# Stick-breaking attention: the weights' small parts on GpSimd by slices, another order of the k products, and the last two key blocks transposed as one group

## The chip, the core and the metric

The kernel runs on one core of a Trainium2 chip. The metric is the device time of one execution in microseconds. The numbers of the trace are those of one profiled execution, from its first to its last instruction. TensorE is PE in the rows (PEld its weight load), VectorE DVE, ScalarE ACT, GpSimd POOL, SyncE SP.

## What is computed

One layer of a macaron block on x of 1024 rows by 1024 columns, in float32: half a SwiGLU feed-forward, stick-breaking attention, half a SwiGLU feed-forward, each with an RMS norm ahead and added to x. The change lies in the attention, with 16 heads of 64 columns:

```python
qkv = (xn @ w_qkv).reshape(b, s, 3, SB_HEADS, SB_HEAD_DIM)
q = rms_norm(qkv[:, :, 0], q_gain).transpose(0, 2, 1, 3)
k = rms_norm(qkv[:, :, 1], k_gain).transpose(0, 2, 1, 3)
v = qkv[:, :, 2].transpose(0, 2, 1, 3)
...
z = jnp.einsum('bhqd,bhkd->bhqk', q[:, :, lo:hi], k[:, :, :hi]) * scale
log_beta = jax.nn.log_sigmoid(z)
log_1m = jnp.where(mask, jax.nn.log_sigmoid(-z), 0.0)
rev = lax.cumsum(log_1m, axis=3, reverse=True)
...
w = jnp.where(mask, jnp.exp(log_beta + rev_excl), 0.0)
outs.append(jnp.einsum('bhqk,bhkd->bhqd', w, v[:, :, :hi]))
```

## The kernel before

Every product in float32 is made of three matmuls of rounded operands: an operand is split into its large part (a copy by ScalarE into the rounded type) and its small part (the operand minus the large part, by VectorE or GpSimd; `split`, L167 to L169). The rows of x are taken in reverse, so a query sees keys from itself onward.

The attention goes pair of heads by pair of heads, p from 0 to 7, after a start that is counted as pair -1. Of a pair there are four units, a head (`hd`, 0 or 1) and a half of 512 queries (`half`). For each unit the scores and the weights are made (`scores`, L747: score matmuls, two sigmoids by ScalarE, a scan by VectorE, a product by GpSimd in L780), and one unit later the weights are transposed and multiplied with v (`values`, L784). `values` takes the key blocks sb from the last to the first: `turn` transposes up to four 128x128 blocks of weights into one PSUM bank and splits them into `th` and `tl`; `apply` multiplies each of the two with v's block into one bank, `bo`. A unit of the later half has 4 key blocks, one of the earlier half 8. The last key block has one 128x128 block of weights, its matmul is 256 wide all the same, and the second 128 columns of `th` and `tl` are set to zero by GpSimd (L801).

Beside the units of pair p run the steps of pair p + 1: its q, k and v (`qkv`, 24 steps of nine matmuls, half 1 first, then half 0), and the loads and splits of the weights of pair p + 2 (`weights_of`: a step loads two 128-row blocks of 384 columns, ScalarE copies 768 columns, GpSimd subtracts 768 columns in one instruction, L659 through L169). When the fourth block of a half is done, `finish` makes the norms' factors (`rsqrt`, VectorE) and GpSimd scales k: the slots 0 and 1 of `qk` are the two heads' q, the slots 2 and 3 their k. L705 writes the second head's k, scaled, into the slots 4 and 5 (512 columns in one instruction), then L708 writes the first head's k into 3 and into 2 (256 columns each). `prep_q` and `prep_k` transpose the slots (`turned_qk`, L725): the first head's keys come from the slots 2 and 3, the second head's from 4 and 5.

The order comes from a plan written out by hand: a pair has 61 units of planned time in four parts a, b, c and d (`PARTS`), every step has a due time, and the steps are traced in the order of these times. From that order the instruction order of each engine is laid out before the run, where an instruction that is expected to be ready may be placed ahead of an earlier one that is not. It is fixed at run time: each engine works its queue in order. In the plan the steps of `qkv` are spread by `FILLS` over the parts; a unit's `turn` steps start 4.0 after a part's start (`TURN`) and each `apply` is due 2.3 after its `turn` (`APPLY`); the keys of the first head and half 0 are due at a + 7.5, those of the second head at b + 8.0, those of half 1 at c + 17.5 and d + 8.0; the weights' steps are due at a + 6, b + 8, d + 2 and d + 8. In pair 6 the mark at d + 16.5 is the place by which the output projection's loads and splits are ordered; they are on SyncE's queue, ScalarE, VectorE and GpSimd.

Of the kernel before, what the change touches and what calls it, by code (L numbers as in the profile page):

```python
# [9 lines left out]
F32 = mybir.dt.float32  # L10
# [7 lines left out]
P = 128  # L18
# [20 lines left out]
PARTS = {"a": 9.0, "b": 14.0, "c": 21.0, "d": 17.0}  # L39
# [4 lines left out]
FILLS = {"a": 3, "b": 6, "c": 8, "d": 7}  # L44
# [54 lines left out]
def macaron_kernel(ctx, tc, x, g1, w1_in, w1_out, gm, w_qkv, gq, gk, w_o, g2, w2_in, w2_out, out):  # L99
# [535 lines left out]
    with ExitStack() as stack:  # L635
# [9 lines left out]
        def weights_of(p, state):  # L645
# [3 lines left out]
            def step(k):  # L649
# [9 lines left out]
                split(raw.rearrange("p k a c -> p k (a c)"), h_[:, ks], l_[:, ks], pool_e)  # L659
                for i in range(2):  # L660
                    wh[k + i], wl[k + i] = h_[:, k % 4 + i, :], l_[:, k % 4 + i, :]
# [3 lines left out]
        def qkv(p, state):  # L665
# [20 lines left out]
            def finish(half, i, ps, room):  # L686
# [16 lines left out]
                rk = r[:, :, 1:2].unsqueeze(3).to_broadcast([P, 4, 2, DH])  # L703
                kv = qk[:, :, 3:4, :].to_broadcast([P, 4, 2, DH])
                pool_e.tensor_tensor(qk[:, :, 4:6, :], kv, rk, op=ALU.mult)  # L705
                for to in (3, 2):
                    rk = r[:, :, 0:1].to_broadcast([P, 4, DH])
                    pool_e.tensor_tensor(qk[:, :, to, :], qk[:, :, 2, :], rk, op=ALU.mult)  # L708
# [31 lines left out]
        def prep_k(state, hd, half):  # L740

            kh_s, kl_s = state["k", hd, half] = [
                pl[f"st{half}"].tile([P, NHALF], F32R, name=f"k{n}_s{half}") for n in "hl"
            ]
            parts(turned_qk(state["qk", half], 2 + 2 * hd), g_sb[1], kh_s, kl_s)
# [38 lines left out]
        def values(state, p, hd, half):  # L784
# [5 lines left out]
            def turn(sb):  # L790
                w = state["w", hd, half]
                n_tb = min(4, sb - tb0 + 1)
                n = n_tb * P
                tp = bank("bt")
                for i in range(n_tb):
                    c = (sb - tb0 - i) * P
                    pe.transpose(tp[:, i * P : (i + 1) * P], w[tb0 + i][:, c : c + P], ident)
                th, tl = now[sb] = [pl["th"].tile([P, NHALF], F32R, name=n) for n in ("th", "tl")]
                if n_tb == 1:
                    for t in (th, tl):  # L800
                        pool_e.memset(t[:, P : 2 * P].bitcast(F32), 0.0)  # L801
                split(tp[:, :n], th[:, :n], tl[:, :n])

            def apply(sb):
                if hd == 0 and sb == NT - 1:
                    state["o", half] = pl["o"].tile([P, NHALF], F32, name=f"o{half}", bufs=1)
                if sb == NT - 1:
                    now["o"] = bank("bo")
                ot = now["o"]
                n = max(min(4, sb - tb0 + 1), 2) * P  # L810
                vv = state["v"][:, sb, 2 * hd : 2 * hd + 2, :].rearrange("p a b -> p (a b)")
                for i, t in enumerate(now.pop(sb)):
# [211 lines left out]
```

## Time and profile before

| | us |
|---|---|
| median of 3 runs | 2016.31 |
| lowest, highest | 2014.38, 2016.91 |
| the profiled execution | 2019.49 |
| its span, first to last instruction | 2017.7 |
| mean granted TensorE clock in it | 0.988 |

The profiled execution has an own time, 1.8 us more than its span. Sums of rows are set against it. In the span the attention's steps run from about 690 to 1316 us, and the pairs 1 to 5, which have all kinds of steps, repeat every 70 to 71 us. A row of a timeline gives in brackets how long the engine was idle before the instruction, and which instruction released it. The granted clock is 1.00 at 2.4 GHz and 0.50 at 1.2 GHz.

### The profile page before, as it was taken

How to read it: one execution, taken by the hardware profiler on the slowest of the kernel's cores; microseconds unless marked ns; L12 is line 12 of the kernel's file. 1: busy time of each engine (PE TensorE's matmuls, PEld its weight loads, DVE VectorE, ACT ScalarE, POOL GpSimd, SP SyncE). 2: the span in 40 equal slices, each digit the busy share in tenths (PEclk: the TensorE clock that was granted, in tenths of full speed). 3: DMA queues.
4: the chain of work that ended last, by engine and by line, in shares of the span. 5: the costliest groups of instructions: out<-in, count | busy, mean ns of one | idle time of the engine just before them, and what ended most of it. 6: DMA issues, size and time to landing. Idle time of an engine off the chain costs nothing.

```text
span 2017.7 us, 27277 instructions
## 1 busy us (share of the span) xinstructions
PE 1926.7 (95%) x9624; PEld 1649.5 (82%) x9624; DVE 1259.7 (62%) x1815; ACT 987.2 (49%) x1828; POOL 1106.3 (55%) x957
## 2 busy tenths in 40 slices
PE   7899999999999789889988998999999999999999
PEld 6788888887888689888888986779888888888887
DVE  6945645636666847767767777567564564547654
ACT  6443443443334457767776777443434334344332
POOL 2567667656456434654555456312766666655554
PEclk9999999999999999999999999999999999999999
DMA  5123233338996410110011013232233233259974
GB/s 204 65 97 111 104 100 103 111 115 294 332 320 222 126 32 6 43 37 27 22 43 32 6 58 126 65 124 69 96 113 100 100 115 99 94 188 360 317 267 150
DMA packets 163031, 251.85 MB, mean 125 GB/s; under 512 B 10960, under 2 KB 80592, under 8 KB 162896
## 3 DMA queue, kind: packets, MB, share of 16 engines
q1 hardware_dynamic: 162896, 250.13, 36.5%
q8 instruction: 75, 1.23, 0.3%
q14 instruction: 60, 0.49, 0.1%
HBM read 193.99 MB, written 56.10 MB: 124 GB/s over the span
## 4 chain that ended last, share of the span: by engine, by line
PE 79%; DVE 10%; POOL 4%; ACT 4%; issue 2%; DMA 1%; POOLq 0%; DVEq 0%; ACTq 0%
PE ka L255 6%; PE ka L256 6%; PE ka L257 6%; PE kc L255 4%; PE kc L256 4%; PE kc L257 4%; PE bq L257 4%; PE bq L255 4%; PE bq L256 4%; PE ma L255 4%; PE ma L256 4%; PE ma L257 4%; PE kb L256 3%; PE kb L255 3%; PE kb L257 3%; PE bo L813 3%
## 5 line engine op out<-in xcount | busy, mean ns | idle before, releaser
L169 POOL TENSOR_TENSOR u<-sf,u 128x512 fp32r<-128x512 f32 x160 | 226.6, 1417 | 160.9 <-ACT u L168 160.1
L169 POOL TENSOR_TENSOR rp<-raw,rp 128x1024 fp32r<-128x1024 f32 x84 | 213.1, 2542 | 184.5 <-ACT rp L168 166.2
L169 POOL TENSOR_TENSOR u<-raw,u 128x512 fp32r<-128x512 f32 x136 | 201.1, 1483 | 147.3 <-ACT u L168 147.2
L780 POOL TENSOR_TENSOR w<-w,om 128x512 f32<-128x512 f32 (+4 forms) x128 | 138.7, 1086 | 134.0 <-DVE om L773 111.1
L168 ACT ACTIVATE u<-sf 128x512 fp32r<-128x512 f32 x160 | 100.9, 630 | 217.8 <-PE kb L256 89.8
L363 DVE TENSOR_TENSOR h<-h 128x512 f32<-128x512 f32 x110 | 134.7, 1228 | 90.0 <-POOL h L464 89.3
L255 PE MATMUL bq<-wqh,xh 128*128 128x384 f32 x512 | 179.2, 350 | 3.8 <-DVE vst L694 3.8
L256 PE MATMUL bq<-wql,xh 128*128 128x384 f32 x512 | 174.2, 340 | 0.0
L257 PE MATMUL bq<-wqh,xl 128*128 128x384 f32 x512 | 173.8, 339 | 0.0
L168 ACT ACTIVATE rp<-rh 128x1024 fp32r<-128x1024 f32 (+1 forms) x78 | 76.6, 984 | 198.6 <-issue 70.8
L255 PE MATMUL ka<-xh,u 128*128 128x512 f32 (+1 forms) x448 | 163.0, 364 | 9.8 <-ACT s L413 7.6
L256 PE MATMUL ka<-xl,u 128*128 128x512 f32 (+1 forms) x448 | 162.8, 364 | 1.2 <-DVE xl L169 1.2
L257 PE MATMUL ka<-xh,u 128*128 128x512 f32 (+1 forms) x448 | 162.3, 362 | 0.0
L485 DVE TENSOR_TENSOR raw<-raw 128x1024 f32<-128x1024 f32 (+1 forms) x60 | 91.0, 1519 | 111.1 <-DMA raw<-w_out 91.0
L168 ACT ACTIVATE u<-raw 128x512 fp32r<-128x512 f32 x136 | 84.6, 631 | 148.2 <-PE ka L256 101.8
L255 PE MATMUL ma<-rp 128*128 128x512 f32 x352 | 138.0, 392 | 2.0 <-DVE h L417 2.0
L771 ACT ACTIVATE w<-bz,f 128x512 f32<-128x512 f32 (+1 forms) x192 | 113.0, 589 | 52.4 <-PE bz L767 50.4
L256 PE MATMUL ma<-rp 128*128 128x512 f32 x352 | 137.6, 391 | 0.0
L257 PE MATMUL ma<-rp 128*128 128x512 f32 x352 | 137.4, 390 | 0.0
L390 DVE TENSOR_TENSOR sf<-raw 128x512 f32<-128x512 f32 x80 | 79.1, 990 | 89.3 <-POOL u L169 88.1
L464 POOL TENSOR_TENSOR h<-h,g 128x512 f32<-128x512 f32 x80 | 112.1, 1401 | 29.0 <-DVE h L417 29.0
L169 DVE TENSOR_TENSOR tl<-bt,th 128x512 fp32r<-128x512 f32 x192 | 103.3, 548 | 33.6 <-ACT th L168 32.8
(220 smaller groups left out, 5584.4 us busy)
## 6 DMA issues: line engine op xcount, KB each, us to landing
raw<-w_out SPq DMA_DIRECT2D x120, 512.0 KB, 5.5
raw<-w_in SPq DMA_DIRECT2D x88, 512.0 KB, 3.6
k<-h SPq DMA_DIRECT2D x154, 256.0 KB, 2.1
rh<-k SPq DMA_DIRECT2D x64, 512.0 KB, 5.8
raw_qkv<-w_qkv SPq DMA_DIRECT2D x64, 192.0 KB, 2.9
x_keep<-x SPq DMA_DIRECT2D x32, 256.0 KB, 2.5
x<-x_keep SPq DMA_DIRECT2D x32, 256.0 KB, 5.0
raw<-w_out SPq DMA_DIRECT2D x24, 256.0 KB, 4.2
```

The source lines that it names most:

```text
L168: act.activation(hi, raw, AF.Copy)
L169: (engine or dve).tensor_tensor(lo, raw, hi.bitcast(F32), op=ALU.subtract)
L255: pe.matmul(dst, ah, bh, start=start and i == 0, stop=False, skip_group_check=onto)
L256: pe.matmul(dst, ah, bl, start=False, stop=False, skip_group_check=onto)
L257: pe.matmul(dst, al, bh, start=False, stop=stop and i == n - 1, skip_group_check=onto)
L363: dve.tensor_tensor(src, hb[of[0]], hb[of[1]], op=getattr(ALU, of[2]))
L390: dve.tensor_tensor(f[n], x, y, op=op)
L464: pool_e.tensor_tensor(h, h, gs[k], op=ALU.mult)
L485: dve.tensor_tensor(w[0], w[0], w[1], op=getattr(ALU, W_OF[m][2]))
L771: act.activation(to, z, AF.Sigmoid, scale=state["f", half][:, sign, tb % 4, hd : hd + 1])
L780: pool_e.tensor_tensor(wt[:, c1 : c0 + n], wt[:, c1 : c0 + n], om[:, c1 - 1 : c0 + n - 1], op=ALU.mult)
L813: pe.matmul(ot[:, :n], vv, t[:, :n], start=sb == NT - 1 and i == 0, stop=sb == tb0 and i == 1)
```

## The change

The constants of the plan: part a gets 10 units instead of 9 and part d 16 instead of 17; a has 4 steps of `qkv` instead of 3 and d has 6 instead of 7. In `weights_of` ScalarE's copy stays one instruction of 768 columns, and GpSimd's subtraction becomes two of 384 columns, each for its own 128-row block. In `finish` the roles of the slots are exchanged: the first instruction (512 columns) now scales the first head's k into the slots 4 and 5, the two of 256 columns scale the second head's k into 2 and 3; `prep_k` takes the slots accordingly. In `values` the last two key blocks form one group: their transposes (two and one, and one of a block of zeros from the tile `first`) go into one bank, one split makes `th` and `tl` of 512 columns, and the four matmuls follow one another. The memsets are gone. A unit has 3 or 7 groups instead of 4 or 8, and the due times of its groups are spread over that number.

```diff
--- before.py
+++ after.py
@@ -36,12 +36,12 @@
 
 
 
-PARTS = {"a": 9.0, "b": 14.0, "c": 21.0, "d": 17.0}
+PARTS = {"a": 10.0, "b": 14.0, "c": 21.0, "d": 16.0}
 PAIR = sum(PARTS.values())
 UNITS = {"a": (1, 1), "b": (0, 0), "c": (1, 0), "d": (0, 1)}
 BEFORE = {"a": (0, 1), "b": (1, 1), "c": (0, 0), "d": (1, 0)}
 
-FILLS = {"a": 3, "b": 6, "c": 8, "d": 7}
+FILLS = {"a": 4, "b": 6, "c": 8, "d": 6}
 
 LOADS = (("a", 6.0), ("b", 8.0), ("d", 2.0), ("d", 8.0))
 
@@ -656,8 +656,11 @@
                 for i in range(2):
                     sp.dma_start(raw[:, i], src[:, i, :, p * P : (p + 1) * P])
                 ks = slice(k % 4, k % 4 + 2)
-                split(raw.rearrange("p k a c -> p k (a c)"), h_[:, ks], l_[:, ks], pool_e)
+                raw = raw.rearrange("p k a c -> p k (a c)")
+                act.activation(h_[:, ks], raw, AF.Copy)
                 for i in range(2):
+                    k_ = k % 4 + i
+                    pool_e.tensor_tensor(l_[:, k_, :], raw[:, i, :], h_[:, k_, :].bitcast(F32), op=ALU.subtract)
                     wh[k + i], wl[k + i] = h_[:, k % 4 + i, :], l_[:, k % 4 + i, :]
 
             return [partial(step, k) for k in ((4, 6, 0, 2) if p == 0 else (0, 2, 4, 6))]
@@ -700,12 +703,12 @@
                 r = pl["sq"].tile([P, 4, 4], F32, name="r", bufs=1)
                 dve.tensor_scalar(r[:, :, 0:2], y[:, :, 2:4], 1.0, None, op0=ALU.mult)
 
-                rk = r[:, :, 1:2].unsqueeze(3).to_broadcast([P, 4, 2, DH])
-                kv = qk[:, :, 3:4, :].to_broadcast([P, 4, 2, DH])
+                rk = r[:, :, 0:1].unsqueeze(3).to_broadcast([P, 4, 2, DH])
+                kv = qk[:, :, 2:3, :].to_broadcast([P, 4, 2, DH])
                 pool_e.tensor_tensor(qk[:, :, 4:6, :], kv, rk, op=ALU.mult)
-                for to in (3, 2):
-                    rk = r[:, :, 0:1].to_broadcast([P, 4, DH])
-                    pool_e.tensor_tensor(qk[:, :, to, :], qk[:, :, 2, :], rk, op=ALU.mult)
+                for to in (2, 3):
+                    rk = r[:, :, 1:2].to_broadcast([P, 4, DH])
+                    pool_e.tensor_tensor(qk[:, :, to, :], qk[:, :, 3, :], rk, op=ALU.mult)
 
                 f = state["f", half] = pl["sq"].tile([P, 2, 4, 2], F32, name=f"f{half}")
                 for n, c in enumerate((0.125, -0.125)):
@@ -742,7 +745,7 @@
             kh_s, kl_s = state["k", hd, half] = [
                 pl[f"st{half}"].tile([P, NHALF], F32R, name=f"k{n}_s{half}") for n in "hl"
             ]
-            parts(turned_qk(state["qk", half], 2 + 2 * hd), g_sb[1], kh_s, kl_s)
+            parts(turned_qk(state["qk", half], 4 - 2 * hd), g_sb[1], kh_s, kl_s)
 
         def scores(state, hd, half):
 
@@ -787,31 +790,39 @@
             tb0 = half * 4
             now = {}
 
-            def turn(sb):
+            def blocks(sb):
+                return min(4, sb - tb0 + 1)
+
+            def turn(sbs):
                 w = state["w", hd, half]
-                n_tb = min(4, sb - tb0 + 1)
-                n = n_tb * P
                 tp = bank("bt")
-                for i in range(n_tb):
-                    c = (sb - tb0 - i) * P
-                    pe.transpose(tp[:, i * P : (i + 1) * P], w[tb0 + i][:, c : c + P], ident)
-                th, tl = now[sb] = [pl["th"].tile([P, NHALF], F32R, name=n) for n in ("th", "tl")]
-                if n_tb == 1:
-                    for t in (th, tl):
-                        pool_e.memset(t[:, P : 2 * P].bitcast(F32), 0.0)
+                n = 0
+                for sb in sbs:
+                    for i in range(max(blocks(sb), 2)):
+                        c = (sb - tb0 - i) * P
+
+                        src = w[tb0 + i][:, c : c + P] if i < blocks(sb) else first[:, P : 2 * P]
+                        pe.transpose(tp[:, n : n + P], src, ident)
+                        n += P
+                th, tl = now[sbs] = [pl["th"].tile([P, NHALF], F32R, name=n) for n in ("th", "tl")]
                 split(tp[:, :n], th[:, :n], tl[:, :n])
 
-            def apply(sb):
-                if hd == 0 and sb == NT - 1:
+            def apply(sbs):
+                if hd == 0 and sbs[0] == NT - 1:
                     state["o", half] = pl["o"].tile([P, NHALF], F32, name=f"o{half}", bufs=1)
-                if sb == NT - 1:
+                if sbs[0] == NT - 1:
                     now["o"] = bank("bo")
                 ot = now["o"]
-                n = max(min(4, sb - tb0 + 1), 2) * P
-                vv = state["v"][:, sb, 2 * hd : 2 * hd + 2, :].rearrange("p a b -> p (a b)")
-                for i, t in enumerate(now.pop(sb)):
-                    pe.matmul(ot[:, :n], vv, t[:, :n], start=sb == NT - 1 and i == 0, stop=sb == tb0 and i == 1)
-                if sb > tb0:
+                c = 0
+                ts = now.pop(sbs)
+                for sb in sbs:
+                    n = max(blocks(sb), 2) * P
+                    vv = state["v"][:, sb, 2 * hd : 2 * hd + 2, :].rearrange("p a b -> p (a b)")
+                    for i, t in enumerate(ts):
+                        start, stop = sb == NT - 1 and i == 0, sb == tb0 and i == 1
+                        pe.matmul(ot[:, :n], vv, t[:, c : c + n], start=start, stop=stop)
+                    c += n
+                if sbs[-1] > tb0:
                     return
                 o = state["o", half]
                 act.activation(o[own, :], ot[other, :], AF.Copy)
@@ -821,8 +832,8 @@
                 elif hd == 1 and (p, half) != (NP - 2, 1):
                     split_o(state, p, half)
 
-            sbs = range(NT - 1, tb0 - 1, -1)
-            return [(partial(turn, sb), partial(apply, sb)) for sb in sbs]
+            groups = [(sb,) for sb in range(NT - 1, tb0 + 1, -1)] + [(tb0 + 1, tb0)]
+            return [(partial(turn, sbs), partial(apply, sbs)) for sbs in groups]
 
         def split_o(state, p, half):
```

## Rows read from the trace of the kernel before

**Rows 1.** The page, part 1: busy us (share of the span) xinstructions.

```profile
PE 1926.7 (95%) x9624; PEld 1649.5 (82%) x9624; DVE 1259.7 (62%) x1815; ACT 987.2 (49%) x1828; POOL 1106.3 (55%) x957
```

**Rows 2.** Stretches: us, busy us (x) of PE, PEld, DVE, ACT, POOL, PEclk, DMA.

```profile
821.00:892.40 71.40, 64.03 (x384) 58.74 (x384) 51.72 (x104) 50.58 (x114) 39.46 (x62) 1.00 0.11 32
```

**Rows 3.** Waits of PE, 700 to 1316: who, whom, us, times, longest.

```profile
PE bz L725 <- POOL qk L708: 20.9, 8, 3.6
PE bo L813 <- POOL tl L801: 9.7, 6, 1.9
...
PE bo L813 <- DVE tl L169: 2.9, 8, 0.6
```

**Rows 4.** Timeline of PE: start us, us, instruction [idle before, releaser], 881 and 892.

```profile
881.24 0.39 PE L813 MATMUL bo<-tl,vst 128*128 128x256 f32 x1 [1.56 <-POOL tl L801]
...
892.78 0.47 PE L725 MATMUL bz<-ident,qk 128*128 128x128 f32 x1 [3.64 <-POOL qk L708]
```

**Rows 5.** Timeline of POOL, 879 to 893, the same columns.

```profile
879.21 1.80 POOL L169 TENSOR_TENSOR wql<-raw_qkv,wqh 128x768 fp32r<-128x768 f32 x1
...
888.50 1.81 POOL L169 TENSOR_TENSOR wql<-raw_qkv,wqh 128x768 fp32r<-128x768 f32 x1
890.27 1.05 POOL L705 TENSOR_TENSOR qk<-qk,r 128x512 f32<-128x512 f32 x1
891.40 0.62 POOL L708 TENSOR_TENSOR qk<-qk,r 128x256 f32<-128x256 f32 x1
```

**Rows 6.** Timeline of DVE, at 887.

```profile
887.44 0.17 DVE L701 TENSOR_SCALAR r<-bq 128x8 f32<-128x8 f32 x1
```

**Rows 7.** Timeline of PE at the keys of four other pairs.

```profile
750.13 1.12 PE L725 MATMUL bz<-ident,qk 128*128 128x128 f32 x4 [4.04 <-POOL w L778]
...
822.94 0.66 PE L725 MATMUL bz<-ident,qk 128*128 128x128 f32 x4 [3.64 <-POOL qk L708]
...
964.17 0.70 PE L725 MATMUL bz<-ident,qk 128*128 128x128 f32 x3 [3.61 <-POOL qk L708]
...
1174.41 0.65 PE L725 MATMUL bz<-ident,qk 128*128 128x128 f32 x4 [1.45 <-POOL qk L708]
```

**Rows 8.** Stretches after a wait, columns as in rows 2 (PEclk: granted clock).

```profile
749.38:756.20 6.82, 6.07 (x22) 5.90 (x23) 1.30 (x3) 1.45 (x4) 2.23 (x7) 0.50 0.22 60
892.74:896.15 3.41, 3.37 (x14) 3.28 (x15) 1.26 (x3) 1.56 (x4) 1.17 (x4) 0.50 0.16 46
822.90:826.30 3.40, 3.36 (x23) 3.24 (x24) 1.28 (x3) 1.34 (x4) 1.60 (x5) 1.00 0.16 45
1234.08:1240.90 6.82, 5.44 (x19) 4.93 (x20) 4.03 (x7) 4.80 (x8) 6.82 (x7) 0.50 0.88 317
```

**Rows 9.** Groups of DVE by shape, 700 to 1316: xcount, busy us, mean ns, idle.

```profile
L773 DVE TENSOR_TENSOR_SCAN om<-bz,om,first 128x512 f32<-128x512 f32 x64 | 82.1, 1282 | 25.0 <-ACT bz L771 22.9
L169 DVE TENSOR_TENSOR tl<-bt,th 128x512 fp32r<-128x512 f32 x96 | 63.8, 682 | 13.4 <-ACT th L168 13.4
```

**Rows 10.** Transposes of PE: their group by shape, then four in a row (timeline).

```profile
L797 PE MATMUL bt<-ident,w 128*128 128x128 f32 x576 | 98.4, 275 | 1.5 <-POOL w L780 1.2
...
872.11 0.60 PE L797 MATMUL bt<-ident,w 128*128 128x128 f32 x4
```

**Rows 11.** Timeline of POOL, 745 to 749.

```profile
745.99 1.05 POOL L705 TENSOR_TENSOR qk<-qk,r 128x512 f32<-128x512 f32 x1
746.99 1.81 POOL L169 TENSOR_TENSOR wql<-raw_qkv,wqh 128x768 fp32r<-128x768 f32 x1
```

**Rows 12.** Groups of POOL by shape, 700 to 1316, columns as in rows 9.

```profile
L780 POOL TENSOR_TENSOR w<-w 128x383 f32<-128x383 f32 x16 | 16.1, 1008 | 10.8 <-DVE w L773 10.8
```

**Rows 13.** Timeline of PE in the last pair.

```profile
1232.97 0.39 PE L813 MATMUL bo<-th,vst 128*128 128x256 f32 x1 [1.64 <-POOL th L801]
...
1235.46 0.58 PE L813 MATMUL bo<-tl,vst 128*128 128x256 f32 x1 [1.87 <-POOL tl L801]
...
1261.60 0.79 PE L256 MATMUL bq<-pa,xh 128*128 128x512 f32 x1 [2.18 <-POOL w L778]
```

## The prediction

> **What bounds the kernel now.** The page's first part comes first: TensorE is busy 95% of the span, the other engines 49 to 62% [rows 1]. So a change that touches GpSimd alone can only pay where TensorE stands still for it. The diff lies in the attention stage, where the heads' pairs follow each other at a fixed pace; in one pair of 71.4 us TensorE is busy 64.0, VectorE 51.7, ScalarE 50.6 and GpSimd 39.5 [rows 2]. The waits of TensorE in the stage name the causes [rows 3]: 20.9 us in 8 waits for the k products (L708), 9.7 us in 6 waits for the memset of the small half (L801). Waits for VectorE's splits are small, 2.9 us in 8.
>
> The timeline shows both in every steady pair, at the same places. Near the end of a unit the last matmul stands 1.56 us before 881.24, and the next pair's first keys stand 3.64 us before 892.78, so from 889.14 [rows 4]. Behind the first lies GpSimd's order: a weights' subtraction of 1.80 us started at 879.21, and the second memset had to wait for its end at 881.01 [rows 5]. Behind the second lies the same: the factors r were ready at 887.44 + 0.17 = 887.61 [rows 6], but a subtraction of 1.81 us began at 888.50, the second head's product (L705, 1.05 us) at 890.27 only, and the first head's two products of 0.62 us followed it, with a 1-column memset between, to 892.72 [rows 5].
>
> **A check that such waits are TensorE's own time.** The keys' wait ends at 822.94, 892.78, 964.17 and 1174.41 in four of the pairs [rows 4, 7]. From 892.78 to 964.17 is 71.4 us, but the last three pairs took 210.2, that is 4.0 less than 3 x 71.4. In the last of them the keys' wait is 1.45 and not 3.64 (2.2 less), and none of the six memset waits lies there (1.56 less): 3.7 of the 4.0. Time taken off these waits comes out at the end.
>
> **The clock behind the waits.** After the wait at 892.78 the granted clock is 0.50 for 3.4 us (1.2 instead of 2.4 GHz), at 749.38 for 6.8; after the equal wait at 822.94 it stayed at 1.00 [rows 8]. What this costs is the difference of two otherwise equal pairs: 892.78 - 822.94 = 69.84 without it and 71.39 with it, so 1.55 us; the pair from 750.13 to 822.94 took 72.81, so 3.0 us for the longer one. Four steady pairs pay 1.55.
>
> **The change, part by part.** The terms are gains, in us of the profiled execution.
>
> Memsets out, last two key blocks together. 64 memsets go from GpSimd. The wait of 1.56 was for one, in 5 steady pairs: 5 x 1.56 = 7.8. What is late next there is the small half from VectorE. The merged group is of the 512-column form, which 96 groups already take at 0.68 us on VectorE [rows 9], planned the same 2.3 units (2.7 us) ahead of its matmuls; all waits for VectorE's small halves sum to 2.9 [rows 3]. 32 more such groups: 32 x 2.9 / 96 = 1.0 lost. The worst of these waits was 0.6, so the bounds are 0 and 20 lost; I take 1.0, since it is the mean of the same form.
> Each of the 32 units (16 heads, two halves) gets one more transpose, of zeros, on TensorE. Four in a row take 0.60, and one alone 0.275 from start to end [rows 10], so (0.60 - 0.275) / 3 = 0.11 each: 3.5 lost, all of it on the path. The Trainium skill, "TensorE: Matmul & The Clock Gate", Part 4, gives about 275 ns for a 128x128 transpose in a kernel. That agrees with one instruction's length here (0.275), and by it the loss would be 8.8 and the time 5 us more; but starts lie 0.11 apart, so the row decides.
>
> First head's k first. Its keys need L705's place alone (1.05) and no longer 1.05 + 2 x 0.62. At 750.13 L705 had started at 745.99 and ended at 747.04, and a subtraction of 1.81 from 746.99 then held up the other two [rows 11]; TensorE came at 750.13 - 4.04 = 746.09 [rows 7], so 1.0 is left: 3.0 gained. At 1174.41 no subtraction is near, and the wait of 1.45 [rows 7] is that of the two products (1.24) and little else: 1.3 gained. Of 20.9 - 5 x 3.63 - 1.45 = 1.3 in the remaining two waits I take 1.0. The second head's keys come later by two small products, but their step is due about 10 plan units after the first's, so those 1.24 us are covered.
>
> Weights slice by slice. No row has the slice itself; the nearest is the product of 383 columns, 1.01 us [rows 12], so two slices take 2.02 where one instruction took 1.80 to 1.85 [rows 5]: 0.2 us more GpSimd time, 32 times, off the path but for the place below. ScalarE's copy and the DMAs stay as they are. In the five steady pairs the subtraction ahead of L705 decides. If both slices stay ahead, the keys come at 888.50 + 2.02 + 1.05 = 891.57 and TensorE, there at 889.14, waits 2.5. If L705 passes the second slice, 1.5. With no slice ahead, near 0. I take 2.0, the middle of the first two, as the order is fixed ahead by expected times and r came only 0.9 ahead of the subtraction: 5 x (3.63 - 2.0) = 8.2, between 5.7 and 18. Sum of the keys' waits: 3.0 + 1.3 + 1.0 + 8.2 = 13.5.
>
> The clock. A wait of 1.0 is shorter than the 1.56 that did not lower it, so 3.0 comes back at 749.38. Waits of 1.5 to 2.5 lie between that and the 3.6 that lowered it in four of five pairs; I take half of 4 x 1.55: 3.1. Together 6.1, bounds 0 and 9.2.
>
> The last pair's start. Two memset waits, 1.64 and 1.87 [rows 13], and 6.8 us at half clock [rows 8] are worth 3.5 + 3.0 = 6.5. But there the output weights' splits fill the other engines and TensorE soon waits for them again, 2.18 at 1261.60; and with a of 10 and d of 16 the mark at d + 16.5 from which those splits and their DMAs are ordered falls one unit (1.2 us) later. I take half: 3.2, bounds 0 and 6.5.
>
> Shifted plan. a grows by a unit and d shrinks, one filling step moves from d to a, and a unit's groups go from 4 or 8 to 3 or 7. Between the last filling step of d and the keys' step of a, three filling and three score steps remain; one turn less and one apply more weigh each other out. Cost nothing, covered by TensorE's own queue; without that cover a shift of a group is some tenths in a pair.
>
> Sum: 7.8 - 1.0 - 3.5 + 13.5 + 6.1 + 3.2 = 26.1. The profiled execution took 2019.5 (span 2017.7 and 1.8 around it), so 1993.4; it lies 0.16% over the median of 2016.3, so 1990 us.
>
> **The rivals.**
> 1. GpSimd's order does not let the first head's keys out earlier: other work takes the freed place, the steady pairs keep 3.6 and the half clock. Then 8.2 and 3.1 fall away: 26.1 - 11.3 = 14.8, some 2001 us. For it: lower work has slipped ahead of these products in every pair. Against: two products of 0.62 no longer stand before those keys, whatever the order.
> 2. More than forecast: L705 ahead of all slices, no wait and no half clock left, the last pair's whole 6.5: 26.1 + 10 + 3.1 + 3.3 = 42.5, some 1974 us. For it: r is ready at 887.61, ahead of the subtraction. Against: the order is fixed before r is known.
> 3. The time is given back: without its waits a pair would be near 66 us, VectorE 51.7 / 66 = 78% busy [rows 2], and the in-order queues of VectorE and ScalarE set the pace at more places. Price: the 26 less a few, some 2012 us, within 0.2%. Against: the pair up to 1174.41 ran at 67.4 with no new wait.
> 4. Slower. The merged group puts all four last matmuls behind one split, which waits for both blocks. If VectorE has one more 512-column scan ahead of the small half (1.28 us [rows 9]) than TensorE has work to cover, each of the 32 units stands for it: 32 x 1.28 = 41, 2016 - 26 + 41 = 2031 us. It decides from 26 / 32 = 0.8 us a group, over the 0.6 that is the worst wait for a small half so far [rows 3]. For it: VectorE is the second busiest in a pair [rows 2]; against: the 96 groups of that form.
>
> **How the numbers follow.** Chances: forecast 0.48 (its own range 1982 to 2000, by the order of the slices and the clock), rival 1 0.20, rival 2 0.10, rival 3 0.12, rival 4 0.10. The range of 1974 to 2010 takes in the forecast, rivals 1 and 2 and the better part of rival 3. Faster by over 0.2% (which is about what can be told from no change) is under 2012.3: 0.48 + 0.20 + 0.10 + 0.03 = 0.81; within it 0.09; slower 0.10.
>
> **What would show it.** In the trace after, no wait for L801; where the unit's last matmuls stood, at most 0.6 for VectorE. The keys' wait between 1.5 and 2.5 in five pairs, after one or two 384-column subtractions of 1.0, and released by the product of 512 columns. A distance of 66 to 67 us between those waits. Half clock in at most two or three pairs, and none near 750. 608 transposes of blocks instead of 576. The forecast is wrong if the keys' wait stays near 3.6, if waits for the merged small half exceed 0.6, or if the distance of the pairs stays over 69.

## The result and the profile after

The changed kernel takes 2000.2 us (median of 4 runs, 1998.8 to 2000.7) against 2016.6 for the kernel before on the same chip: a ratio of 0.9913, 95% interval 0.9898 to 0.9928. The profiled execution took 2000.7 us with a span of 1998.7, where the one before had 2019.5 and 2017.7: 18.8 us less by execution. Forecast were 1990 us and 26.1 us less. In the changed kernel the product of 512 columns is L708, the two small ones are L711, the keys are turned at L728, memset and product of the weights are L781 and L783, the group is turned at L805 and applied at L823.

The page, part 1 (busy us, share of the span, instructions), answering [rows 1]: 32 matmuls more, 32 instructions fewer on VectorE, ScalarE and GpSimd each.

```profile
PE 1928.4 (96%) x9656; PEld 1651.5 (83%) x9656; DVE 1260.4 (63%) x1783; ACT 988.3 (49%) x1796; POOL 1100.9 (55%) x925
```

The waits of TensorE from 700 to 1316 us, answering [rows 3] (who, for whom, us in total, times, longest):

```profile
PE bz L728 <- POOL qk L708: 12.2, 6, 2.4
PE bq L257 <- POOL w L781: 4.1, 1, 4.1
PE bt L805 <- POOL w L783: 3.6, 9, 1.2
...
PE bo L823 <- DVE tl L169: 1.6, 5, 0.6
PE bo L823 <- ACT th L168: 1.5, 1, 1.5
```

No wait for a memset of the small half is left (9.7 us before), nor the 1.6 for one of the large half. The keys are waited for 12.2 us instead of 20.9 and the 4.0 at 750 us. Waits for VectorE's small halves fell from 2.9 to 1.6. Against that stand waits that are new or have grown: 1.5 for ScalarE's large half, 4.1 in the last pair (0.6 before), 3.6 in nine waits for GpSimd's product of the weights, L783 (1.2 in one before), and three new ones of 0.4 to 0.8. At the keys, timeline of TensorE and then of GpSimd (start, us, instruction, idle before and releaser), answering [rows 4, 5, 7]:

```profile
740.41 0.49 PE L823 MATMUL bo<-th,vst 128*128 128x512 f32 x1 [1.47 <-ACT th L168]
...
879.23 0.66 PE L728 MATMUL bz<-ident,qk 128*128 128x128 f32 x4 [2.30 <-POOL qk L708]
```
```profile
877.17 1.00 POOL L663 TENSOR_TENSOR wql<-raw_qkv,wqh 128x384 fp32r<-128x384 f32 x1
878.12 1.05 POOL L708 TENSOR_TENSOR qk<-qk,r 128x512 f32<-128x512 f32 x1
879.13 1.01 POOL L663 TENSOR_TENSOR wql<-raw_qkv,wqh 128x384 fp32r<-128x384 f32 x1
880.09 1.33 POOL L711 TENSOR_TENSOR qk<-qk,r 128x256 f32<-128x256 f32 x2
```

The product of 512 columns stands between the two slices, and the keys are released by it. The stretches behind these waits, answering [rows 8] (us, busy us of PE, PEld, DVE, ACT, POOL, then the granted clock):

```profile
742.16:745.57 3.41, 3.41 (x16) 3.41 (x15) 3.35 (x7) 3.04 (x8) 3.41 (x7) 0.50 0.39 112
810.43:813.84 3.41, 3.41 (x14) 3.41 (x15) 1.86 (x4) 1.60 (x4) 2.80 (x5) 0.50 0.29 82
878.70:882.10 3.40, 2.87 (x20) 2.87 (x21) 2.39 (x6) 1.73 (x5) 3.32 (x7) 1.00 0.27 79
...
1216.62:1226.86 10.24, 6.78 (x24) 5.49 (x24) 7.71 (x18) 4.14 (x9) 7.88 (x10) 0.50 0.92 329
1240.51:1247.34 6.83, 6.13 (x18) 4.89 (x18) 3.02 (x5) 1.84 (x4) 3.30 (x5) 0.50 0.44 148
```

Behind the shorter waits the clock is still 0.50 (1.2 instead of 2.4 GHz) at 810, 947, 1015 and 1083 us, at 1.00 only at 879; in the last pair 17.1 us are at half clock, where before it was 10.2 us.

**One measure for all kernels.** I take the stretch from the first turn of q and k (720.17 before, 715.47 after) to the first product behind the attention (1852.96 and 1834.17). The row of the whole stretch (us, busy us as above):

```profile
720.17:1852.96 1132.79, 1080.96 (x5687) 940.50 (x5686) 727.14 (x1185) 631.41 (x1276) 613.68 (x669) 0.99 0.25 83
```
```profile
715.47:1834.17 1118.70, 1085.07 (x5720) 944.66 (x5718) 729.72 (x1153) 632.40 (x1244) 606.76 (x629) 0.98 0.25 84
```

The length less TensorE's busy time is its idle time: 51.8 us before, 33.6 after. So 18.2 us of waits went away, but TensorE was busy 4.1 us longer; together 14.1. The other 4.7 of the 18.8 lie ahead of the stretch, which started 4.70 us sooner. A second trace of the kernel before, below, has such an early start without the change.

| kernel | stretch, us | gained | idle | at half clock | median, us | ratio, 95% |
|---|---|---|---|---|---|---|
| before | 1132.8 | - | 51.8 | 30.7 | 2016.6 | 1 |
| before, second trace | 1133.1 | -0.3 | 51.6 | 30.7 | | |
| slices alone | 1133.7 | -0.9 | 50.0 | 41.0 | 2016.1 | 0.9979 to 1.0001 |
| new plan alone | 1132.8 | 0.0 | 52.2 | 30.7 | 2018.1 | 0.9992 to 1.0011 |
| merged groups alone | 1124.9 | 7.9 | 42.6 | 37.5 | 2012.2 | 0.9957 to 0.9985 |
| key order alone | 1117.5 | 15.3 | 40.8 | 17.1 | 2003.9 | 0.9908 to 0.9944 |
| order + merged | 1108.0 | 24.8 | 31.3 | 20.5 | 1992.5 | 0.9852 to 0.9900 |
| ... + new lengths | 1121.1 | 11.7 | 41.1 | 34.1 | 2005.0 | 0.9926 to 0.9964 |
| ... + filling steps | 1117.0 | 15.8 | 34.5 | 27.3 | 1999.6 | 0.9896 to 0.9953 |
| ... + both (no slices) | 1122.3 | 10.5 | 38.4 | 30.7 | 2005.5 | 0.9913 to 0.9960 |
| order + merged + slices | 1111.8 | 21.0 | 32.6 | 27.3 | 1999.1 | 0.9876 to 0.9924 |
| the change, all four | 1118.7 | 14.1 | 33.6 | 34.1 | 2000.2 | 0.9898 to 0.9928 |
| the change, mark earlier | 1118.2 | 14.6 | 34.3 | 30.7 | 2000.3 | 0.9909 to 0.9947 |
| order + merged, keys later | 1100.4 | 32.4 | 27.0 | 10.2 | 1988.2 | 0.9844 to 0.9876 |

Idle is length less busy time; half clock is the sum of the stretches with a granted clock of 0.50 inside it. Each ratio is against the kernel before on the same chip. The other columns are of one profiled execution each. That the stretch repeats within 0.3 us is shown for the kernel before alone; differences of a few us between other rows are believed here only where the waits in the rows account for them.

Half clock costs busy time. Two pairs of the changed kernel, one with 3.4 us of it and one without:

```profile
810.39:879.23 68.84, 65.84 (x388) 60.80 (x389) 51.64 (x99) 51.03 (x110) 37.34 (x55) 0.98 0.10 31
879.23:946.34 67.11, 64.25 (x389) 59.26 (x389) 51.72 (x100) 50.78 (x110) 37.26 (x55) 1.00 0.11 32
```

TensorE is busy 1.6 us longer, 0.47 us for each us at half clock. Between whole kernels this holds only roughly: 11.7 us for 23.9 between the change and the last row of the table, but 3.3 for 13.6 between order + merged and the same with the new lengths.

### The profile page after: what moved, and what is told of

The parts are those of the page before. It is cut to its first block, busy times and chain, and to the rows that moved or that the text cites. A ratio compares the mean times of both kernels' runs of the same rounds, so it can differ in the third digit from the quotient of the medians.

```text
span 1998.7 us, 27230 instructions
## 1 busy us (share of the span) xinstructions
PE 1928.4 (96%) x9656; PEld 1651.5 (83%) x9656; DVE 1260.4 (63%) x1783; ACT 988.3 (49%) x1796; POOL 1100.9 (55%) x925
## 3 DMA queue, kind: packets, MB, share of 16 engines
q8 instruction: 75, 1.23, 0.3%
## 4 chain that ended last, share of the span: by engine, by line
PE 79%; DVE 7%; POOL 5%; ACT 5%; issue 2%; DMA 2%; SPq 0%; ACTq 0%; DVEq 0%; POOLq 0%
PE ka L255 6%; PE ka L256 6%; PE ka L257 6%; PE kc L255 4%; PE kc L256 4%; PE kc L257 4%; PE ma L255 3%; PE ma L257 3%; PE ma L256 3%; PE kb L255 3%; PE kb L256 3%; PE kb L257 3%; PE bq L257 3%; PE bq L256 3%; PE bq L255 3%; PE bo L823 3%
## 5 line engine op out<-in xcount | busy, mean ns | idle before, releaser
L783 POOL TENSOR_TENSOR w<-w,om 128x512 f32<-128x512 f32 (+4 forms) x128 | 138.6, 1088 | 126.9 <-DVE om L776 98.0
L169 DVE TENSOR_TENSOR tl<-bt,th 128x512 fp32r<-128x512 f32 (+1 forms) x160 | 105.1, 657 | 32.0 <-ACT th L168 29.9
```

Source lines behind the costliest of these rows:

```text
L169: (engine or dve).tensor_tensor(lo, raw, hi.bitcast(F32), op=ALU.subtract)
L783: pool_e.tensor_tensor(wt[:, c1 : c0 + n], wt[:, c1 : c0 + n], om[:, c1 - 1 : c0 + n - 1], op=ALU.mult)
```

## The experiments

**The four edits, each alone in the kernel before.** First the slices:

```diff
-                split(raw.rearrange("p k a c -> p k (a c)"), h_[:, ks], l_[:, ks], pool_e)
+                raw = raw.rearrange("p k a c -> p k (a c)")
+                act.activation(h_[:, ks], raw, AF.Copy)
                 for i in range(2):
+                    k_ = k % 4 + i
+                    pool_e.tensor_tensor(l_[:, k_, :], raw[:, i, :], h_[:, k_, :].bitcast(F32), op=ALU.subtract)
```

> The kernel before with GpSimd's subtraction of the weights in two slices of 384 columns, and nothing else of the change. In the trace of after, TensorE is 4.7 us ahead of before by the transposes at the end of the first feed-forward (710 us), which no term of the prediction held. Theory A (VectorE stands behind GpSimd): before, small VectorE instructions with two SBUF inputs take 1.68 to 1.80 us instead of 0.16 while a 768-column subtraction runs, so the slices alone bring 4 to 5 us by 715 us; the memset waits shrink from 1.56 to about 0.6 as only one slice stands ahead (5 x 0.9); the keys' waits stay near 3.7, since GpSimd's order keeps both slices ahead of the products. Sum 8 to 10, some 2007 us. Theory B (the start moved for another reason, as the plan's constants): nothing by 715 us, 2 to 5 in all, some 2013 us.

Measured 2016.1: both numbers missed. The stretch is 0.9 us longer. The five memset waits of 1.56 us did shrink, to 0.7 for VectorE's v at the same place, but the keys' waits did not stay: they grew to 3.9 to 4.2 in the steady pairs (3.64 before), and half clock from 30.7 to 41.0 us. Their line:

```profile
PE bz L728 <- POOL qk L711: 23.0, 8, 4.2
```

The trace did start 5.2 us sooner at the first turn of q and k, as I had expected, but it lost about as much again at the end, at 1994 us, and neither has to do with the slices (below).

```diff
...
-                    rk = r[:, :, 0:1].to_broadcast([P, 4, DH])
-                    pool_e.tensor_tensor(qk[:, :, to, :], qk[:, :, 2, :], rk, op=ALU.mult)
+                    rk = r[:, :, 1:2].to_broadcast([P, 4, DH])
+                    pool_e.tensor_tensor(qk[:, :, to, :], qk[:, :, 3, :], rk, op=ALU.mult)
...
-            parts(turned_qk(state["qk", half], 2 + 2 * hd), g_sb[1], kh_s, kl_s)
+            parts(turned_qk(state["qk", half], 4 - 2 * hd), g_sb[1], kh_s, kl_s)
```

> The kernel before with the first head's k scaled first, and nothing else of the change. GpSimd's order is else the same, a whole subtraction of 768 columns ahead of the products. Theory of the prediction: the keys' wait falls by the two products, 3.63 to 2.4 in five pairs (6.2), 1.45 to 0 (1.3), 1.0 in the start, and from 4.04 to 1 in pair 0 with its 6.8 us at half clock (3.0 + 3.0); half clock stays in the steady pairs as waits of 2.4 lower it too. Sum 12 to 15, some 2003 us. Rival (given back): the waits shrink, but others in the queues of ScalarE and VectorE take their place: 3 to 6 us, some 2012 us. Nothing by 715 us in either.

Measured 2003.9, as expected. Its waits, and stretches at its keys:

```profile
PE bz L725 <- POOL qk L705: 12.8, 7, 2.3
PE bo L813 <- POOL tl L801: 9.7, 6, 1.9
```
```profile
815.51:818.92 3.41, 3.34 (x21) 2.93 (x22) 1.36 (x4) 1.34 (x4) 2.76 (x8) 1.00 0.42 115
885.65:889.06 3.41, 3.41 (x13) 3.29 (x13) 1.28 (x3) 0.78 (x4) 1.55 (x6) 0.50 0.19 56
954.42:957.83 3.41, 3.35 (x21) 2.94 (x22) 1.37 (x4) 1.34 (x4) 2.76 (x8) 1.00 0.40 115
1023.25:1026.66 3.41, 3.35 (x21) 2.94 (x22) 1.37 (x4) 1.34 (x4) 2.75 (x8) 1.00 0.40 115
```

The keys' wait is 2.24 in the steady pairs instead of 3.64, and the memset waits stay (9.7 us). The clock was expected to stay at half behind such waits and did not: it is at 1.00 behind four of the five. Nearly the same wait, 2.1 to 2.4, had half clock behind it in four of five pairs of the changed kernel. What decides between them isn't settled.

The merged groups alone (the block of `values` from the diff):

> The kernel before with the last two key blocks as one group and zeros transposed instead of memsets, and nothing else of the change. Theory of the prediction: 7.8 from five memset waits, 3.5 at the last pair's start, less 3.5 for 32 transposes and 1.0 for waits on VectorE: 4 to 7, some 2011 us; keys' waits stay 3.6 with half clock in four pairs. Rival (small half comes late): each unit waits 0.4 to 0.7 for the merged small half, the gain is eaten, 2014 to 2022 us.

Measured 2012.2, as expected. The memset waits are gone; the keys' wait stays at 3.4 to 3.7 with half clock behind each.

```diff
-PARTS = {"a": 9.0, "b": 14.0, "c": 21.0, "d": 17.0}
+PARTS = {"a": 10.0, "b": 14.0, "c": 21.0, "d": 16.0}
-FILLS = {"a": 3, "b": 6, "c": 8, "d": 7}
+FILLS = {"a": 4, "b": 6, "c": 8, "d": 6}
```

> The kernel before with the new lengths of the parts a and d and the new filling steps, and nothing else of the change. Theory A (neutral): within 3 us of before, 2014 to 2019, TensorE's stops the same in number and size. Theory B (the mark of pair 6 falls one unit later and delays the output weights): the stage from the last pair's start (about 1233 to 1270 in before) loses 4 to 7 us, as in the trace of after, where 27 us ahead became 20; 2020 to 2023 us.

Measured 2018.1: no effect on the time. It hides two that roughly cancel, though: in the five steady pairs the keys' wait grew from 3.64 to 4.03, and the memset's shrank from 1.56 to 1.07.

**Two at a time.** The parts add up to 22.3 us in the stretch, the change has 14.1. So some of them spoil each other, and combinations had to tell which. Order and merged groups together, all else as before:

> The key order and the merged last groups together, with the old part sizes and the whole small parts of the weights. Counted from the first turn of q and k (about 715 us) to the first product after the attention (about 1850 us), the order alone gained 15.3 us over the kernel before, the merged groups alone 7.9, the slices -0.9, the part sizes 0.0, sum 22.3; the changed kernel gained 14.1. Theory A (the new part sizes cost the last pair's start some 4 us once the pairs are shorter, and the slices another 1 to 4): the two edits add up, 23 us in this stretch, about 1994 us. Theory C (order and merged groups take the same waits away, and the late keys stay the end of both): 15 to 16 us, about 2002 us. Which it is, is read from the waits ahead of the turned keys (2.2 us in the order alone, 3.5 in the merged groups alone) and from the stretches at half clock.

The two add up as theory A says: 24.8 us in the stretch (the sum of the two is 23.2), 1992.5 us, 8 us less than the change with all four edits. Next the change with the old plan, and the change without slices:

> The changed kernel with the part sizes of the kernel before (9, 14, 21, 17 and 3, 6, 8, 7). Theory A: the 4.1 us wait for the last weights' block at 1219 us, and the 17 us at half clock around it, shrink to what the order alone shows there (0.85 us; 13.7 us at half clock in two stretches): 4 us less, about 1996 us. Theory C: the wait stays or moves on, 1999 to 2001 us.

> The changed kernel with each small part of a weight in one subtraction of 768 columns again. If the slices brought the 4.7 us by which the changed kernel was ahead at 715 us, they are lost: about 2005 us. If that start is a matter of the execution (the merged groups alone were 5.5 us ahead there without any slices, the slices alone 5.2), the time moves by under 2 us: 1998 to 2002 us. My forecast of step one was no effect of the slices but for the place where the keys' 512-column product passes one; without slices that product waits for a whole 1.8 us subtraction or goes ahead of it, and the wait for the keys is 1.5 to 3.3 us.

The old plan gives 21.0 in the stretch instead of 14.1, so the new plan costs 6.9 beside the other edits. Its median of 1999.1 hardly shows it; its profiled execution lost 6.2 us behind the attention. The reason given in theory A fails: the wait at the last weights does not shrink to 0.85, a wait of 4.60 for GpSimd's product of the weights stands in its place. Without slices 10.5 are left; the 2005.5 us look like the first theory's 2005, but the first turn of q and k comes 1.5 us later and not 4.7 (716.92 against 715.47), and 3.6 us are lost in the stretch. With the new plan the slices gain these 3.6, with the old one they lose 24.8 - 21.0 = 3.9. A good part of both is in the keys' waits of the five steady pairs: with the new plan 2.1 to 2.4 us with slices and 2.8 to 2.95 without, with the old one 2.4 to 2.65 with and 2.0 to 2.3 without. The reason is in GpSimd's order. With the old plan both slices stay ahead of the product of 512 columns (timeline of GpSimd, then TensorE's keys):

```profile
875.19 1.96 POOL L663 TENSOR_TENSOR wql<-raw_qkv,wqh 128x384 fp32r<-128x384 f32 x2
877.11 1.05 POOL L708 TENSOR_TENSOR qk<-qk,r 128x512 f32<-128x512 f32 x1
```
```profile
878.21 0.33 PE L728 MATMUL bz<-ident,qk 128*128 128x128 f32 x1 [2.37 <-POOL w L781]
```

With the new plan the product stands between them, as shown above at 878.12.

**The two halves of the new plan**, each added to order and merged groups (the first or the second line of its diff):

> Key order and merged groups (24.8 us gained between the first turn of q and k and the first product after the attention, 1992.5 us) plus the new lengths of the parts alone (10, 14, 21, 16; filling steps as before). With both halves of the new plan, and without slices, 10.5 us were left of the 24.8. Theory P (the lengths: unit d now ends half a plan unit ahead of the mark at d + 16.5, and the output weights' work starts later): the wait near 1219 us grows from 0.85 to about 3.5 us, as with both, and at least half of the 14.3 us is lost here, 2000 us or more. Theory F (the moved filling step): under 4 us lost here, 1993 to 1996 us.

> Key order and merged groups plus the new numbers of filling steps alone (4, 6, 8, 6; lengths as before). Theory F: one more filling step between the products of the second head and the first keys of a pair changes GpSimd's and TensorE's order in every pair; the wait for the keys grows from 2.1 to about 2.8 us and at least half of the 14.3 us is lost here, 2000 us or more. Theory P: under 4 us lost, 1993 to 1996 us.

Each costs: the lengths 13.1 us of the stretch, the filling steps 9.0, both together 14.3 and not 22.1. So both theories get their loss, but not by their reasons: the lengths' trace has no wait for splits near 1219 us, and with the filling steps the keys' wait is 2.3 to 2.5 and not 2.8. The lengths work at the keys. GpSimd and TensorE at the keys with the old lengths (order and merged groups), then with the new ones:

```profile
877.84 1.82 POOL L169 TENSOR_TENSOR wql<-raw_qkv,wqh 128x768 fp32r<-128x768 f32 x1
879.62 1.05 POOL L705 TENSOR_TENSOR qk<-qk,r 128x512 f32<-128x512 f32 x1
```
```profile
878.11 0.34 PE L257 MATMUL bq<-wqh,xl 128*128 128x384 f32 x1
880.72 0.33 PE L725 MATMUL bz<-ident,qk 128*128 128x128 f32 x1 [2.28 <-POOL w L778]
```
```profile
874.77 1.81 POOL L169 TENSOR_TENSOR wql<-raw_qkv,wqh 128x768 fp32r<-128x768 f32 x1
876.53 1.05 POOL L705 TENSOR_TENSOR qk<-qk,r 128x512 f32<-128x512 f32 x1
```
```profile
873.61 0.27 PE L802 MATMUL bt<-ident,w 128*128 128x128 f32 x1
877.64 0.47 PE L725 MATMUL bz<-ident,qk 128*128 128x128 f32 x1 [3.76 <-POOL qk L705]
```

GpSimd does the same in the same time; TensorE is at the keys 1.5 us sooner and waits 3.76 instead of 2.28, and half clock follows in all five steady pairs, 23.9 us in sum, where it was four of five and 13.7. What TensorE no longer has ahead of the keys stands in its rows: with the old lengths the last thing before them is a filling step, from 877.14 to 878.45, and with the new ones it is a turn of weights; the filling step comes behind the keys, at 879.83. (It is one of six matmuls; of three filling steps two have nine and the third has six.) The due times in the code say the same. Of three filling steps the third is due at 7.5 in a part of 9, ahead of the keys at a + 7.5, and at 8.33 in a part of 10, behind them. With four filling steps in a part of 10 the third is due at 6.25, ahead again, and with both halves of the plan the keys' wait is 2.8 to 2.95. What differs from the filling steps alone, with their 2.3 to 2.5, is then the unit's third turn: it stands ahead of the keys there, at 877.59, and with both halves behind them, at 881.47 (due at 7.33 and 8.0).

Of the 9.0 us of the filling steps 3.6 are in the last pair: from the keys at about 1150 to the end of the stretch it takes 683.9 us with them (1151.56 to 1835.50), 680.9 with the new lengths (1154.15 to 1835.01), 680.3 with neither (1147.70 to 1828.02). The other 5.4 lie ahead of it, 2.1 in waits and 3.3 in busy time at the same 13.7 us of half clock; their cause stays open.

**The keys' step later.** If the keys are waited for because their step comes too early on TensorE, it can be moved:

```diff
-                put("a", 7.5, partial(prep_k, this, 0, 0))
+                put("a", 9.0, partial(prep_k, this, 0, 0))
```

> Key order and merged groups, and the step that turns the first head's keys 1.5 plan units (about 1.8 us) later in its unit. Theory of the clock and the keys: the waits of 2.0 to 2.3 us in five pairs shrink to about 0.4, 5 x 1.8 = 9 us, and with them goes most of the half clock behind them (3.4 us in four pairs, 1.55 us each by the rows of the kernel before, 6 us): 1977 us. Rival: the work that is put ahead of the keys was needed later to cover the wait for the scores' scans, and TensorE stands there instead: 1988 to 1994 us.

Measured 1988.2 us, the fastest of all: a ratio of 0.986 to the kernel before, at the near end of the rival's span. The rival's mechanism is not seen in the steady pairs, which have no new wait over 0.5 us. The wait shrank to 1.2 to 1.5 us, not to 0.4, and the stretch is 7.6 us shorter than without the move. The half clock is gone from all steady pairs:

```profile
877.41 0.33 PE L725 MATMUL bz<-ident,qk 128*128 128x128 f32 x1 [1.28 <-POOL w L778]
```
```profile
877.41:880.82 3.41, 3.41 (x21) 3.27 (x22) 1.93 (x4) 1.41 (x3) 2.39 (x5) 1.00 0.44 120
...
877.41:943.46 66.05, 64.24 (x389) 59.40 (x389) 51.68 (x100) 50.60 (x110) 36.85 (x50) 1.00 0.11 33
```

The last row also bears on the added transposes. A pair at full clock with the old groups (key order alone):

```profile
815.51:884.39 68.88, 64.36 (x384) 58.70 (x385) 51.08 (x103) 50.54 (x114) 37.94 (x58) 1.00 0.11 31
```

TensorE is busy 64.24 us with four transposes of zeros more, and 64.36 without: no cost can be seen. But pairs at full clock scatter by 0.5 us, as much as the four would cost at 0.11 each: 64.03 in the kernel before [rows 2], 63.86 to 64.39 in the others. So this bounds the cost and does not measure it.

**The mark.** The changed kernel with the mark one unit earlier:

```diff
-                put("d", 16.5, lambda: marks.append(tc.cur_priority))
+                put("d", 15.5, lambda: marks.append(tc.cur_priority))
```

> The changed kernel with the mark at d + 15.5 in place of d + 16.5, so that it lies as far ahead of the end of unit d as in the kernel before. Theory: the splits of the output weights and of the kept outputs start a unit (1.2 us) earlier on GpSimd, the wait of 4.1 us at 1219 us shrinks to about 1, and with it some of the 17 us at half clock around it: 4 us, about 1996 us. Rival (these splits are behind because the pairs became shorter, not because of the mark): under 1.5 us, 1999 to 2001 us.

The rival holds: 2000.3 us, 0.5 us in the stretch. The wait at the last weights is 3.36 instead of 4.11, and what went there came back right behind it, as a wait of 1.60 for VectorE's scan. The rows of the changed kernel, TensorE and GpSimd, say why:

```profile
1219.31 0.80 PE L257 MATMUL bq<-pb,xl 128*128 128x512 f32 x1 [4.11 <-POOL w L781]
```
```profile
1208.01 2.39 POOL L169 TENSOR_TENSOR pb<-raw,pb 128x1024 fp32r<-128x1024 f32 x1
...
1210.82 2.39 POOL L169 TENSOR_TENSOR pb<-raw,pb 128x1024 fp32r<-128x1024 f32 x1
1213.16 6.09 POOL L169 TENSOR_TENSOR xl<-raw,xh 128x1024 fp32r<-128x1024 f32 x2
```

The releaser named, a memset at 1219.20, is only the instruction behind these splits; by the program TensorE waits for the last of them (`xl`), which ended at 1219.25, and GpSimd had no gap ahead of it.

**The start.** The kernel before once more, unchanged:

> The kernel before, unchanged, for a second trace. If the start of 4.7 us is a matter of the execution, the product on VectorE at about 651 us (2.72 us in the first trace, after a wait of 1.04 us for its load) takes 1.22 us in some executions of this kernel too, and the first turn of q and k is then at about 715 instead of 720 us. If it belongs to the slices, it is 2.7 us long and at 720 us again. About 2017 us.

2014.3 us, the first turn of q and k at 714.41 instead of 720.17. What differs at 650 us is one product on VectorE and a subtraction on GpSimd beside it, first in the first trace, then in the second:

```profile
650.87 2.40 POOL L169 TENSOR_TENSOR rp<-rh,rp 128x1024 fp32r<-128x1024 f32 x1
...
651.64 2.72 DVE L485 TENSOR_TENSOR raw<-raw 128x1024 f32<-128x1024 f32 x1 [1.04 <-DMA raw<-w_out]
```
```profile
649.98 1.23 DVE L485 TENSOR_TENSOR raw<-raw 128x1024 f32<-128x1024 f32 x1 [0.17 <-DMA raw<-w_out]
...
650.09 3.40 POOL L169 TENSOR_TENSOR rp<-rh,rp 128x1024 fp32r<-128x1024 f32 x1
```

So a start that is 5 us early is a matter of the execution, and the theory that the slices bring it falls. The merged groups alone, which have no slices, were 5.6 us ahead there too. That it all comes of whether the load lands just before or just after GpSimd begins is argued, not shown: GpSimd's subtraction is 0.8 us sooner already, and between 673 and 709 us the first trace has 10.2 us at half clock, the second 3.4. Behind the attention the same product costs some executions a wait of 3.3 us and a stretch of half clock: the traces of slices alone, merged groups alone, order + merged + slices, and order + merged + filling steps have it (between 1974 and 1994 us), the others 1.0 us or nothing. This may be why the medians of kernels with four runs scatter by some us, and it is why the table goes by the stretch.

## Why the forecast was right or wrong

The direction and the range held: 2000.2 lies in 1974 to 2010, and in the forecast's own 1982 to 2000 but for 0.2. The reasons hold for two of the four edits and fail for a third. 4.7 us of the 18.8 are luck, so 14.1 stand against 26.1 (the medians differ by 16.4).

- **Memsets out: 7.8 forecast, right.** The five waits of 1.56 are gone; merged groups alone gained 7.9. The merged small half was to cost 1.0 and brought 1.3 (2.9 to 1.6). So rival 4, slower by late small halves, had nothing: the longest such wait is 0.6, below its 0.8.
- **Zero transposes: 3.5 forecast lost, none seen.** 0.44 a pair was forecast, and the pairs at full clock differ by no more than their scatter (64.24 against 64.36). By the Trainium skill's 275 ns each ("TensorE: Matmul & The Clock Gate", Part 4) an estimate would be 1.1 a pair; these pairs leave no room for that, as the four stand in a row with the others.
- **Keys: 13.5 forecast, 12.7 measured** (20.9 + 4.0 - 12.2). The wait near 750 went, the one at 1174 too, and five waits of 2.1 to 2.4 are left, released by the product of 512 columns, in the span of 1.5 to 2.5. In place of the wait near 750, though, TensorE waits 1.47 us for ScalarE at 740.
- **The clock: 6.1 forecast, 1.6 measured: mis-sized.** "I take half of 4 x 1.55" failed: four steady pairs had half clock before and four have it after. Only the first pair gave 3.4 us of half clock back, 1.6 us at 0.47. In the second trace of the kernel before not even that: its first pair has 3.4 us and all five steady pairs have half clock, with the same 30.7 in sum. So after an equal wait the clock differs between executions of one kernel. The key order alone lost the half clock in all but one pair, so a wait of 2.3 can go either way. Two signs of the forecast failed with this: half clock in two or three pairs at most and none near 750 (it is there at 742), and pairs 66 to 67 us apart (67.1 to 68.8).
- **The last pair's start: 3.2 gained forecast, 5.9 lost.** From the keys at 1174.41 to the end of the stretch it took 678.6 us before, and 684.4 from 1149.75 after. This is the term that failed most. The two memset waits went, and TensorE then stood for the splits on GpSimd, 4.1 us, at half clock for 17.1 us instead of 10.2. I had named this ("TensorE soon waits for them again") and still taken half the gain. Even order and merged groups alone take 680.3 there, with a wait of 4.60 for a product that GpSimd does behind such splits; 3.6 more come with the filling steps, not with the mark, which I had blamed.
- **The shifted plan, "cost nothing", failed.** It costs nothing alone (0.0) but 6.9 us beside the other three edits, 4.6 ahead of the last pair's keys and 2.2 behind. Only 1.1 of this is wait; 5.8 is busy time, of which 6.8 us more at half clock explain 3.2, and the rest stays open. Without the slices more of it is wait, and its place is known. My count of steps ahead of the keys was not wrong in number, but "weigh each other out" was: the keys' step is fixed at a + 7.5 in a part that grows, so the unit's third turn falls behind the keys, and the wait is 0.4 to 0.6 us longer a pair (2.8 to 2.95 with both halves of the plan and no slices, 2.3 to 2.5 with the filling steps alone). In the change a slice that comes behind the product takes this back at the keys, but not the half clock.
- **The slices, off the path but for one place: the place was right.** Passing the second slice or not goes with the sign: 3.6 gained with the new plan, 3.9 lost with the old one.

By idle and busy time: 18.2 us of idle went where the terms had some 22 (7.8 - 1.0 + 13.5 and half of 3.5); busy time should have fallen by 4 (6.1 + half of 3.0 - 3.5), and it rose by 4.1. So two thirds of the gap of 12.0 lie in busy time. The keys of the last pair divide the stretch in two; before, then after:

```profile
720.17:1174.41 454.24, 417.37 (x2448) 383.69 (x2447) 323.61 (x657) 321.52 (x724) 239.24 (x368) 0.98 0.11 34
1174.41:1852.96 678.55, 663.59 (x3239) 556.82 (x3240) 403.54 (x529) 309.89 (x552) 374.45 (x302) 0.99 0.34 116
```
```profile
715.47:1149.75 434.28, 417.85 (x2470) 385.97 (x2468) 323.95 (x631) 321.19 (x696) 233.25 (x340) 0.98 0.11 36
1149.75:1834.17 684.42, 667.22 (x3251) 558.70 (x3250) 405.77 (x523) 311.21 (x549) 373.51 (x289) 0.99 0.34 115
```

Ahead of these keys 20.0 us were gained: 20.4 of waits, less 0.5 of busy time. Behind them 5.9 were lost: 2.2 of waits and 3.6 of busy time, of which the 6.8 us more at half clock explain 6.8 x 0.47 = 3.2. Ahead, 3.4 us less at half clock should have taken off 1.6; the 2.1 us of busy time over that stay open. The added transposes are not it: order + merged has them too and is busy 413.6 us there with 13.7 us at half clock, 3.7 less than the kernel before, where 6.8 us less of half clock give 3.2.

Rival 1 gave 2001 us and meets the time, but not by its mechanism: it has the steady waits at 3.6, and they are 2.3. Its other half, the half clock that stays, is what happened. Rival 3 (given back at other places) happened in part: the last pair, the new wait at 740, and the waits for GpSimd's product of the weights, 2.4 us more in all.

## What to carry to other kernels

When several edits go in together, run the ones that seem to pay without those that seem to cost nothing: here two edits alone are 8 us faster than all four, in part because steps that are spread over a part's length moved past one with a fixed due time, and TensorE had less work ahead of its wait. A wait that is shortened but left may keep its half clock; moving the waiting step later, so that the wait fell under 1.5 us, brought 7.6 us, where cutting up the work ahead of its producer brought between -3.9 and 3.6. And where one execution is compared with one other, compare the stretch that the change touches, since starts differ by 5.8 us in the same kernel and ends by 5 to 6 between kernels that are the same there.

## What was not expected of the hardware

Two instructions, one on VectorE and one on GpSimd, each with two inputs from SBUF, don't run side by side in these traces. The product on VectorE takes 1.23 us when it starts at 649.98, before GpSimd's subtraction at 650.09, and that one takes 3.40 instead of 2.40 us. When it starts at 651.64, 0.77 us into the subtraction, it takes 2.72 and ends 1.09 us after it. The Trainium skill, "SBUF — State Buffer", section "SBUF: two separate sides", says that the two engines share a port pair and that whichever starts first keeps it for the whole instruction; both pairs of rows agree. The price here is 1.5 us at the product; the first turn of q and k, 5.8 us later in the one trace than in the other, holds more than that.
